# Gates ahead of q and k in the first projections of a two-layer retention trunk

## The chip, the cores and the metric

The kernel runs on one core of a Trainium2 chip. The core has a matrix engine (PE, with its weight loads listed apart as PEld), a vector engine (DVE), a scalar engine (ACT), a general engine (POOL) and an engine that issues the transfers (SP). They run their own instruction lists and wait for each other through semaphores. Matmuls write to PSUM, which has eight banks of 128 x 512 float32.

The metric is the time of one execution on the device, in microseconds. The kernel before takes 1574.14 us, the median of three runs (1573.3 to 1576.88).

## The reference, cut to what matters

Two layers over 512 tokens with 1024 channels. The part in which the change lies is the first layer's input projection and the retention behind it:

```python
h = modulate(rmsnorm(x, norm1[l]), sh1, sc1)
proj = h @ w_in[l]
q, k, v, g_sw, p_in, gates = jnp.split(proj, IN_SPLITS, axis=-1)
q = rotary(q.reshape(bsz, s, RET_HEADS, RET_QK_DIM), cos, sin)
k = rotary(k.reshape(bsz, s, RET_HEADS, RET_QK_DIM), cos, sin)
v = v.reshape(bsz, s, RET_HEADS, RET_V_DIM)
ret = head_rmsnorm(retention_chunkwise(q, k, v)).reshape(bsz, s, RET_V)
ret_d = (jax.nn.silu(g_sw) * ret) @ w_ret_o[l]
# ... the pooling branch, the merge, the output projection and the feed-forward part
```

There are 8 heads with 64 channels of q and k and 128 channels of v and of `g_sw`. In the kernel "gate" means a 128-column tile of `g_sw`, one for each head, with its SiLU. A 128-column tile of q or k holds two heads.

## The kernel before, in words

**Numbers and tiles.** Every float32 matrix product is done as three products of a split form: each operand is a high part (`whi` for weights) and a low part (`wlo`), and high x high, low x high and high x low are summed in PSUM (`mm3`). A weight chunk is 128 x 1024 (eight units of 128 x 128); it is fetched into `raw` (4 buffers), cast to `whi` and subtracted to `wlo` (5 buffers each). `ps()` takes one of the 8 PSUM banks. `h` holds the eight normalised input tiles, `tab` (4 buffers) the cosine and sine tables of the rotary step, `t` temporaries, `r` longer-lived tiles.

**The first projections** (`start`, line 670). While the modulation rows of layer 0 still arrive, the loop over the eight input tiles k makes `h[k]`, fetches weight chunk k and adds its products into eight PSUM banks at once: two tiles of q, two of k and four gates (`N_GATES`). Within one k the eight tiles are written one after another, in the order of the list `cols`, once for each of the three products. All eight banks are taken when the loop ends.

**What follows it.** For head group g = 0 (heads 0 to 3) the program runs through q pair 0, q pair 1, k pair 0, k pair 1: `tile_of` hands out the PSUM tile, `rotary` (line 750) copies it out in four 32-row pieces on ACT (`COPY t<-ps`), multiplies the bank by the cosine table on DVE (`t<-ps,tab`), multiplies the copy by the sine table and adds. Then each half is cast to `r` on ACT and the rest is subtracted on DVE. The four gates come after that: one `ACTIVATE r<-ps` with SiLU each (`gate`, line 788). Then the v projection (`vp`, line 820) takes four banks at once and runs 8 x 4 x 3 = 96 matmuls over them; in the trace these are `ps<-whi,h` and `ps<-wlo,h`. Then, head by head, the scores (`ps<-r,r` and `ps<-ql,r`), the projection of the gate of a later head, and the product with v (`ps<-s,r`).

**What sets the order.** The body only records operations; `Recorder.order` then plays a list schedule. Matmuls keep the order in which they were recorded. On the other engines it takes what is ready, by due times that it works out backwards from the matmuls that need a result and from the next user of a buffer. A PSUM bank is given to the tiles in the order of their first use, and each new tile takes the bank that comes free first. The planner also decides which of DVE and POOL, or of ACT and DVE, runs some operations. Each engine then executes its list strictly in that order, with SP's list of transfers among them. Accesses of two engines to the same PSUM bank are kept apart by semaphores in the order of that plan, reads too.

Since every operation is emitted by one line, the profile calls all of them L384; tiles are told apart by name.

Of the kernel before, what the change touches and what calls it, by code (L numbers as in the profile page):

```python
# [14 lines left out]
P = 128  # L15
# [4 lines left out]
HEADS = 8  # L20
# [13 lines left out]
C_G = C_V + D  # L34
# [14 lines left out]
N_GATES = 4  # L49
# [346 lines left out]
def trunk(ctx, tc, xT, cin, wada, vecs, wst, rot, trid, icnt, out):  # L396
# [8 lines left out]
    def ps():  # L405
        return nc.tile(pp, [P, S], F32, "ps", 8)
# [64 lines left out]
    def unit(l, name, k, col, n=1):  # L471
        key = (l, name, k, col)
        if key not in order:
            for q in range(n):
                order[(l, name, k, col + q * P if n > 1 else col)] = len(order)
        c, o = divmod(order[key], UNITS)
        for cc in range(c, c + look[0] + 1):
            prep(cc)
        sl = slice(o * P, (o + n) * P)
        return his[c][:, sl], los[c][:, sl]  # L480

    def mm3(out_ap, w, a, start, stop):

        (wh, wl), (ah, al) = w, a
        for n, (s, m) in enumerate(((wh, ah), (wl, ah), (wh, al))):
            nc.tensor.matmul(out_ap, lhsT=s, rhs=m, start=start and n == 0, stop=stop and n == 2)
# [10 lines left out]
    def hs(h, sl):  # L497
        return tuple(z[:, sl] for z in h)
# [20 lines left out]
    def mod_tile(l, t):  # L519

        w = raw_tile()
        nc.sync.dma_start(out=w, in_=wada[l, t])
        nc.vector.scalar_tensor_tensor(
            out=w, in0=w, scalar=1.0, in1=cact, op0=ALU.mult, op1=ALU.mult, accum_out=mods[l][:, t:t + 1],
        )

    def mod_bias(l, t0, n):
        m, b0 = mods[l], V_B + l * 48 + t0
        nc.vector.tensor_add(out=m[:, t0:t0 + n], in0=m[:, t0:t0 + n], in1=vec[:, b0:b0 + n])
# [56 lines left out]
    def make_h(l, which, k, sl, h):  # L586

        hh, hl = (z[:, sl] for z in h)
        sh = mods[l][:, (0 if which == 1 else 24) + k:][:, :1]
        t = temp()[:, sl]  # L590
        nc.vector.scalar_tensor_tensor(
            out=t, in0=x[k][:, sl], scalar=gains[l, which][:, k:k + 1], in1=rs[:, sl], op0=ALU.mult, op1=ALU.mult)
        nc.add({
            "scalar": ("activation", (hh, t, AF.Identity), dict(bias=sh)),
            "vector": ("tensor_scalar", (), dict(out=hh, in0=t, scalar1=sh, scalar2=None, op0=ALU.add)),
        })
        nc.vector.scalar_tensor_tensor(
            out=hl, in0=t, scalar=sh, in1=hh.bitcast(F32), op0=ALU.add, op1=ALU.subtract)

    def new_h():  # L600
        return [tuple(nc.tile(ap, [P, S], F32R, "h", N_H) for _ in range(2)) for _ in range(KT)]

    def first_tiles(l, which, h, name, cols, norm_b):

        o = [ps() for _ in cols]
        for sl in (A, B):
            for k in range(KT):
                for t, c in zip(o, cols):
                    mm3(t[:, sl], unit(l, name, k, c), hs(h[k], sl), k == 0, k == KT - 1)
                if sl is A and k == STAT_AT:  # L610
                    norm_b()
                    for kk in range(KT):
                        make_h(l, which, kk, B, h[kk])
        return o
# [31 lines left out]
    h = new_h()  # L646
# [7 lines left out]
    def first_norm():  # L654

        ss = [(sl, ps()[:, sl]) for sl in (A, B)]
        for n in range(N_WARM):
            nc.tensor.matmul(ss[1][1][:, :P], lhsT=ones, rhs=ones, start=True, stop=True)
        silu_c()
        q = []  # L660
        for k in range(KT):
            q.append(square(k))
            if 0 < k < KT - 2:
                nc.vector.tensor_add(out=q[0], in0=q[0], in1=q.pop())
        for sl, o in ss:
            for n in range(3):
                nc.tensor.matmul(o, lhsT=ones, rhs=q[n][:, sl], start=n == 0, stop=n == 2)
        return ss

    def start(cols):  # L670

        ss = first_norm()
        o = [ps() for _ in cols]
        for k in range(KT):
            mod_tile(0, 8 + k)
            mod_tile(0, k)
            mod_bias(0, k, 1)
            mod_bias(0, 8 + k, 1)
            gain(0, 1, k, 1)
            prep(k, 2 if k == 0 else 1)  # L680
            for sl in (A, B) if k == 0 else (FULL,):
                if k == 0:
                    rstd(rs[:, sl], dict(ss)[sl], D)
                make_h(0, 1, k, sl, h[k])
            nc.urgent = False
            if k + 1 == KT:
                look[0] = LOOK
            for sl in (A, B) if k == 0 else (FULL,):
                for n, (a, b) in enumerate(((0, 0), (1, 0), (0, 1))):
                    for t, c in zip(o, cols):  # L690
                        nc.tensor.matmul(t[:, sl], lhsT=unit(0, "in", k, c)[a], rhs=h[k][b][:, sl],
                                         start=k + n == 0 and sl.start != S // 2, stop=k + n == KT + 1)
        nc.sync.dma_start(out=ic, in_=icnt)
        nc.sync.dma_start(out=tri, in_=trid)
        return o

    def qk_cols(t):

        g, r = divmod(t, 4)
        is_k, pair = divmod(r, 2)  # L700
        return is_k * RQK + (2 * g + pair) * P
# [58 lines left out]
    norm_b = None  # L760
    for l in range(DEPTH):
# [2 lines left out]
        gates = {}  # L764
        p0 = {}
        if l == 0:
            done = start([qk_cols(t) for t in range(4)] + [C_G + n * P for n in range(N_GATES)])
        else:
            done = first_tiles(l, 1, h, "in", [qk_cols(t) for t in range(3)], norm_b)
        fill = [("gate", n) for n in range(len(done) - 4 if l == 0 else 0, HEADS)] + [("pool", g) for g in (3, 2, 1, 0)]  # L770

        def tile_of(col, mid=None):
            if done:
                return done.pop(0)
            o = ps()
            project(o, l, "in", col, h, mid=mid)
            return o
# [10 lines left out]
        def gate(hd):  # L788
            gp = tile_of(C_G + hd * P)
            gates[hd] = keep(F32)  # L790
            nc.scalar.activation(gates[hd], gp, AF.Silu)

        for g in range(2):

            parts = []
            for is_k in (0, 1):
                for p in range(2):
# [6 lines left out]
                    o = rotary(pr, tab)  # L804
# [10 lines left out]
                            nc.vector.tensor_sub(out=ql[own], in0=o[own], in1=z[own].bitcast(F32))  # L815
                            parts.append([z, ql])

            for n in range(len(done)):
                gate(n)
            vp = [ps() for _ in range(4)]  # L820
            for k in range(KT):
                wv = unit(l, "in", k, C_V + g * 512, 4)
# [5 lines left out]
            for i in range(4):  # L828
# [4 lines left out]
                for j in range(4):  # L833
                    c0 = min(j, 2) * P
                    w = S - c0
                    o = sp[min(j, 2)][:, w * (j == 3):w * (j == 3) + w]
# [41 lines left out]
        for j in range(KT):  # L878
            o = ps()
# [17 lines left out]
        for j in range(KT):  # L897
# [6 lines left out]
            t = temp()  # L904
# [15 lines left out]
        norm_b = close(l, "out", 0, merged, 16, STAT_TILES["out"], half_a)  # L920


        done = first_tiles(l, 2, h2, "ffn_in", [0, FF, P], norm_b)
# [19 lines left out]
        if l + 1 < DEPTH:  # L943
# [3 lines left out]
            h = new_h()  # L947
# [18 lines left out]
        norm_b = close(l, "ffn_out", HALF_FT, hid, 40, STAT_TILES["ffn_out"], half_a, l + 1 == DEPTH)  # L966
# [69 lines left out]
```

## Time and profile before

| what | value |
|---|---|
| median of three runs | 1574.14 us (1573.3 to 1576.88) |
| the profiled execution's own time | 1580.4 us |
| its span, first to last instruction | 1578.6 us |
| PE busy | 1537.1 us (97%), 7302 matmuls |
| DVE, ACT, POOL busy | 894.2 (57%), 557.5 (35%), 168.9 us (11%) |
| mean granted PE clock | 0.988 |
| DMA | 201.18 MB, mean 127 GB/s |

The span is the time from the first to the last instruction of one profiled execution; 1.8 us of its own time lie outside the span, and the execution was 6.3 us slower than the median of the runs. A busy share is an average over the whole program; a place where PE stands still is seen in the views by stretch of time. In rows of the timeline the first two numbers are the start and the duration in us, `x8` is the number of instructions merged into the row, and a bracket gives the idle time before it and what ended that. PEclk is the clock that PE was granted, 1.00 being full speed.

### The profile page before, as it was taken

To read this page: it belongs to the slowest core of one execution; us is meant where nothing else is said; L and a number is where in the kernel's file an instruction comes from. 1 tells how busy PE (TensorE), PEld (TensorE's weight loads), DVE (VectorE), ACT (ScalarE), POOL (GpSimd) and SP (SyncE) were. 2 spreads that over 40 slices of the span, in tenths; PEclk is the share of its full clock that TensorE was granted. 3 is DMA by queue.
4 is the path that set the end of the run, shared out by engine and by line. 5 is a ranking of instruction groups with operands and counts; after the bars stand their busy time and mean duration, and the time that the engine had idled before them with its cause. 6 is when DMAs were issued, how large, how long until landed. Compare 5 with 4: busy or idle time off the path is not lost.

```text
span 1578.6 us, 18373 instructions
## 1 busy us (share of the span) xinstructions
PE 1537.1 (97%) x7302; PEld 1280.5 (81%) x7302; DVE 894.2 (57%) x1284; ACT 557.5 (35%) x784; POOL 168.9 (11%) x130
## 2 busy tenths in 40 slices
PE   7899999999999999999999999999999999999997
PEld 5678878888988888888898888888889888888887
DVE  8957785377485434654377766546747433333344
ACT  3355653232342222222256666223224322122222
POOL 2211351000010000000021323100002000000000
PEclk8989999999999999999999999999999999999999
DMA  7742424466245434564224232445622333332321
GB/s 242 253 138 64 149 58 145 152 200 195 70 146 163 142 94 147 187 189 155 84 75 154 80 107 67 147 146 186 202 94 74 101 96 102 96 93 94 94 67 54
DMA packets 59305, 201.18 MB, mean 127 GB/s; under 512 B 6609, under 2 KB 8913, under 8 KB 59218
## 3 DMA queue, kind: packets, MB, share of 16 engines
q1 hardware_dynamic: 59218, 200.00, 40.1%
q8 instruction: 57, 0.93, 0.2%
q14 instruction: 30, 0.25, 0.0%
HBM read 197.87 MB, written 2.10 MB: 127 GB/s over the span
## 4 chain that ended last, share of the span: by engine, by line
PE 91%; DVE 6%; ACT 1%; DMA 1%; issue 1%; DVEq 0%; SPq 0%; ACTq 0%
PE ps L384 91%; DVE t L384 3%; DVE raw L384 1%; DVE h L384 1%; ACT t L384 1%; DMA xall<-xT 0%; DVE r L384 0%; DVE mod L384 0%; DMA raw<-wst 0%; DVE acc L384 0%; DVE xall L384 0%; DVE s L384 0%; ACT whi L384 0%; DVE rs L384 0%; DVE wlo L384 0%
## 5 line engine op out<-in xcount | busy, mean ns | idle before, releaser
L384 PE MATMUL ps<-h,whi 128*128 128x512 f32 (+1 forms) x2720 | 812.6, 382 | 14.4 <-DVE h L384 11.6
L384 PEld LDWEIGHTS ps<-h,whi 128*128 128x128 f32 x2720 | 502.0, 189 | 117.0 <-DVE h L384 11.4
L384 DVE TENSOR_TENSOR wlo<-raw,whi 128x1024 fp32r<-128x1024 f32 (+1 forms) x233 | 290.3, 1248 | 380.7 <-ACT whi L384 380.0
L384 PE MATMUL ps<-h,wlo 128*128 128x512 f32 (+1 forms) x1360 | 504.5, 379 | 0.0
L384 ACT CAST whi<-raw 128x1024 fp32r<-128x1024 f32 (+1 forms) x239 | 250.4, 1048 | 688.9 <-PE ps L384 486.3
L384 PE MATMUL ps<-r,whi 128*128 128x512 f32 (+1 forms) x1620 | 442.3, 357 | 0.0
L384 PEld LDWEIGHTS ps<-r,whi 128*128 128x128 f32 x1620 | 286.9, 188 | 46.6
L384 PEld LDWEIGHTS ps<-h,wlo 128*128 128x128 f32 x1360 | 255.8, 189 | 49.5
L384 PE MATMUL ps<-r,wlo 128*128 128x512 f32 (+1 forms) x810 | 288.1, 356 | 0.0
L384 PEld LDWEIGHTS ps<-r,wlo 128*128 128x128 f32 x810 | 152.2, 188 | 23.0
L384 POOL TENSOR_TENSOR wlo<-raw,whi 128x1024 fp32r<-128x1024 f32 x29 | 72.9, 2517 | 620.0 <-DVE rs L384 329.1
L384 DVE SCALAR_TENSOR_TENSOR raw<-raw,cact 128x1024 f32<-128x1024 f32 x96 | 122.4, 1277 | 13.6 <-DMA raw<-wada 13.1
L384 PE MATMUL ps<-whi,h 128*128 128x512 f32 x256 | 83.5, 408 | 8.6 <-ACT t L384 8.6
L384 DVE TENSOR_TENSOR t<-ps,t 128x512 f32<-128x512 f32 x60 | 41.3, 688 | 78.9 <-PE ps L384 78.2
L384 DVE SCALAR_TENSOR_TENSOR xall<-ps,mod,xall 128x512 f32<-128x512 f32 (+1 forms) x62 | 39.0, 628 | 71.8 <-PE ps L384 71.8
L384 ACT ACTIVATE t<-ps 128x512 f32<-128x512 f32 x76 | 45.0, 595 | 89.9 <-PE ps L384 89.9
L384 PEld LDWEIGHTS ps<-whi,h 128*128 128x128 f32 x256 | 49.3, 194 | 22.6 <-ACT t L384 10.9
L384 DVE TENSOR_TENSOR r<-t,r 128x512 fp32r<-128x512 f32 (+1 forms) x76 | 56.2, 740 | 5.3 <-ACT r L384 3.3
L384 ACT CAST r<-t 64x512 fp32r<-64x512 f32 (+1 forms) x84 | 51.6, 617 | 18.8 <-DVE t L384 16.0
L384 PE MATMUL ps<-wlo,h 128*128 128x512 f32 x128 | 51.8, 405 | 0.0
L384 ACT ACTIVATE sq<-xall 128x256 f32<-128x256 f32 (+1 forms) x42 | 20.5, 488 | 85.2 <-DVE xall L384 79.5
L384 ACT COPY t<-ps 32x512 f32<-32x512 f32 (+1 forms) x72 | 41.5, 578 | 25.2 <-PE ps L384 18.2
(89 smaller groups left out, 848.8 us busy)
## 6 DMA issues: line engine op xcount, KB each, us to landing
raw<-wst SPq DMA_DIRECT2D x261, 512.0 KB, 3.6
raw<-wada SPq DMA_DIRECT2D x96, 512.0 KB, 4.1
tab<-rot SPq DMA_DIRECT2D x32, 256.0 KB, 3.7
xall<-xT SPq DMA_DIRECT2D x4, 512.0 KB, 6.7
out<-t SPq DMA_DIRECT2D x7, 256.0 KB, 2.4
out<-t SPq DMA_DIRECT2D x2, 128.0 KB, 2.3
tri<-trid SPq DMA_DIRECT2D x1, 128.0 KB, 4.7
vec<-vecs SPq DMA_DIRECT2D x1, 72.0 KB, 7.7
```

The source lines that it names most:

```text
L384: getattr(eng, method)(*[real(a) for a in args], **{k: real(v) for k, v in kw.items()})
```

## The change

The list of columns in `start` begins with the four gates, and the two tiles of q and two of k follow. `start` returns a dictionary by column instead of a list, so that `tile_of` finds each tile by its column. The gates that `start` made are handled before the loop over head groups, so ahead of the rotary steps of q and k, where before they stood between the rotary steps and the v projection. In layer 1, which has no gates among its first tiles, only the bookkeeping changes. Nothing that is computed changes, and neither does the number of matmuls, transfers or SiLU calls.

```diff
@@ start
-        return o
+        return dict(zip(cols, o))
@@ trunk, at the head of each layer
         if l == 0:
-            done = start([qk_cols(t) for t in range(4)] + [C_G + n * P for n in range(N_GATES)])
+            done = start([C_G + n * P for n in range(N_GATES)] + [qk_cols(t) for t in range(4)])
         else:
-            done = first_tiles(l, 1, h, "in", [qk_cols(t) for t in range(3)], norm_b)
-        fill = [("gate", n) for n in range(len(done) - 4 if l == 0 else 0, HEADS)] + [("pool", g) for g in (3, 2, 1, 0)]
+            cols = [qk_cols(t) for t in range(3)]
+            done = dict(zip(cols, first_tiles(l, 1, h, "in", cols, norm_b)))
+        fill = [("gate", n) for n in range(N_GATES if l == 0 else 0, HEADS)] + [("pool", g) for g in (3, 2, 1, 0)]
 
         def tile_of(col, mid=None):
-            if done:
-                return done.pop(0)
+            if col in done:
+                return done.pop(col)
...
+        for n in range(HEADS):
+            if C_G + n * P in done:
+                gate(n)
         for g in range(2):
...
-            for n in range(len(done)):
-                gate(n)
             vp = [ps() for _ in range(4)]
```

How the instruction lists differ is seen at two places. In the rows below a name is tile, buffer and a running number: `ps_4` is PSUM bank 4, and the bracket names the engines or transfer queues whose semaphores the instruction waits for.

The first is ACT just after its last weight cast for the v projection. `ps_4` to `ps_7` are the four tiles that `start` takes first (the q and k tiles before, the gates now), `ps_1`, `ps_2`, `ps_3` and `ps_0` the other four. Before:

```order
L384 CAST whi_1_572<-raw_3_550 128x1024 [waits DMAHW2_49,PE_49,Pool_49]
L384 COPY t_7_596<-ps_4_190 32x512 [waits PE_49]
L384 COPY t_7_596<-ps_4_190 32x512 [waits DVE_49]
L384 COPY t_7_596<-ps_4_190 32x512 x2
L384 COPY t_5_615<-ps_5_195 32x512 [waits PE_49]
L384 COPY t_5_615<-ps_5_195 32x512 [waits DVE_49]
L384 COPY t_5_615<-ps_5_195 32x512 x2
L384 COPY t_6_634<-ps_6_197 32x512 [waits PE_49]
```

And now:

```order
L384 CAST whi_1_570<-raw_3_548 128x1024 [waits DMAHW1_49,PE_49,Pool_49]
L384 ACT_TABLE_LOAD
L384 ACTIVATE r_0_596<-ps_4_190 128x512 [waits PE_49]
L384 ACTIVATE r_1_601<-ps_5_195 128x512 [waits PE_49]
L384 ACTIVATE r_2_606<-ps_6_197 128x512 [waits PE_49]
L384 ACTIVATE r_3_615<-ps_7_200 128x512 [waits PE_49]
L384 COPY t_7_623<-ps_1_202 32x512 [waits DVE_49,PE_49]
L384 COPY t_7_623<-ps_1_202 32x512
L384 COPY t_7_623<-ps_1_202 32x512 [waits DVE_49]
L384 COPY t_7_623<-ps_1_202 32x512
```

The table load and the four SiLU calls, which stood behind all 16 copies and all 12 casts of the rotary steps, now stand ahead of them; the rotary pieces moved behind.

The second is PE at the first matmuls of the v projection. Before:

```order
L384 MATMUL ps_4_619<-whi_3_524,h_0_188 128x512 [waits DVE_49,Activation_49]
L384 MATMUL ps_4_619<-whi_3_524,h_1_211 128x512
L384 MATMUL ps_4_619<-wlo_3_562,h_0_188 128x512
L384 MATMUL ps_5_636<-whi_3_524,h_0_188 128x512 [waits DVE_49,PE_49,Activation_49]
L384 MATMUL ps_5_636<-whi_3_524,h_1_211 128x512
L384 MATMUL ps_5_636<-wlo_3_562,h_0_188 128x512
L384 MATMUL ps_6_653<-whi_3_524,h_0_188 128x512 [waits DVE_49,PE_49,Activation_49]
L384 MATMUL ps_6_653<-whi_3_524,h_1_211 128x512
L384 MATMUL ps_6_653<-wlo_3_562,h_0_188 128x512
L384 MATMUL ps_7_673<-whi_3_524,h_0_188 128x512 [waits PE_49,Activation_49]
```

And now:

```order
L384 MATMUL ps_4_608<-whi_3_522,h_0_188 128x512 [waits Activation_49]
L384 MATMUL ps_4_608<-whi_3_522,h_1_211 128x512
L384 MATMUL ps_4_608<-wlo_3_560,h_0_188 128x512 [waits DVE_49]
L384 MATMUL ps_5_618<-whi_3_522,h_0_188 128x512 [waits Activation_49]
L384 MATMUL ps_5_618<-whi_3_522,h_1_211 128x512
L384 MATMUL ps_5_618<-wlo_3_560,h_0_188 128x512
L384 MATMUL ps_6_628<-whi_3_522,h_0_188 128x512 [waits Activation_49]
L384 MATMUL ps_6_628<-whi_3_522,h_1_211 128x512
L384 MATMUL ps_6_628<-wlo_3_560,h_0_188 128x512
L384 MATMUL ps_7_633<-whi_3_522,h_0_188 128x512 [waits Activation_49]
```

The banks are the same four, but their former content is now a gate, which one SiLU on ACT reads, and no longer a q or k tile, which four copies on ACT and a product on DVE read. The order of the matmuls themselves is the same in the whole program but for the tiles that change places within `start`. On ACT, DVE, POOL and SP the two lists differ only around the rotary steps and the first head of layer 0 (6 to 24 rows an engine); POOL has two instructions fewer, DVE two more.

## The prediction

> **What bounds the kernel now.** I read the page first, then what PE waits for, then stretches of time.
>
> ```profile
> span 1578.6 us, 18373 instructions
> PE 1537.1 (97%) x7302; PEld 1280.5 (81%) x7302; DVE 894.2 (57%) x1284; ACT 557.5 (35%) x784; POOL 168.9 (11%) x130
> ```
>
> PE is busy 97% of the span, so only places where PE stands still or runs slowly can give time. The waits of PE, as engine, tile, what was waited for, us in total, times, longest:
>
> ```profile
> PE ps L384 <- DVE h L384: 11.6, 9, 3.0
> PE ps L384 <- ACT t L384: 8.6, 4, 2.9
> ```
>
> The second row is what the change touches: four waits for a rotary copy. The view by stretch shows where it lies (columns: length, busy us and instructions of each engine, granted clock, DMA share, GB/s):
>
> ```profile
> core 0: us, PE busy (x) PEld busy (x) DVE busy (x) ACT busy (x) POOL busy (x), PEclk, DMA share, GB/s
> 57.00:73.20 16.20, 14.23 (x60) 10.75 (x59) 15.10 (x19) 5.83 (x6) 5.72 (x2) 1.00 0.86 271
> 73.10:76.03 2.93, 0.00 (x1) 0.00 (x0) 1.70 (x3) 1.75 (x4) 0.00 (x0) 1.00 0.88 316
> 76.03:91.21 15.18, 9.49 (x21) 6.28 (x22) 10.07 (x14) 12.61 (x22) 5.11 (x4) 0.55 0.72 236
> 91.21:108.70 17.49, 17.49 (x76) 14.03 (x75) 7.44 (x9) 8.70 (x13) 0.00 (x0) 1.00 0.30 91
> 108.70:117.66 8.96, 8.96 (x46) 7.50 (x44) 5.92 (x14) 3.35 (x7) 2.41 (x1) 1.00 0.20 59
> 131.00:200.00 69.00, 69.00 (x313) 56.39 (x311) 50.63 (x71) 41.39 (x66) 22.96 (x16) 1.00 0.35 107
> 228.00:235.00 7.00, 5.17 (x18) 4.37 (x19) 6.00 (x12) 4.03 (x8) 3.35 (x2) 0.76 0.25 75
> ```
>
> Between the last matmul of the first projections and the first score lies the v projection. Its first 15.18 us hold little work and run at a clock of 0.55; the rest runs full. The rows of PE there:
>
> ```profile
> 71.10 2.00 PE L384 MATMUL ps<-h,whi 128*128 128x512 f32 x8
> 76.03 0.74 PE L384 MATMUL ps<-whi,h 128*128 128x512 f32 x2 [2.93 <-ACT t L384]
> 79.14 1.22 PE L384 MATMUL ps<-whi,h 128*128 128x512 f32 x2 [2.13 <-ACT t L384]
> 82.25 1.22 PE L384 MATMUL ps<-whi,h 128*128 128x512 f32 x2 [1.46 <-ACT t L384]
> 85.99 1.22 PE L384 MATMUL ps<-whi,h 128*128 128x512 f32 x2 [2.09 <-ACT t L384]
> 107.31 0.63 PE L384 MATMUL ps<-whi,h 128*128 128x512 f32 x2
> 108.00 0.63 PE L384 MATMUL ps<-whi,h 128*128 128x512 f32 x2
> 108.70 0.39 PE L384 MATMUL ps<-r,r 128*128 128x512 f32 x1
> ```
>
> The first projections end at 71.10 + 2.00 = 73.10. Each of v's four banks is waited for separately, because its former q or k tile has to be copied out first. From 73.10 to the first score at 108.70 it takes **35.60 us**. At full clock three matmuls take 108.70 − 108.00 = 0.70 us (and 108.00 − 107.31 = 0.69), so v's 96 need 32 x 0.70 = 22.4 us. The other 13.2 us are idle time (8.61, the sum of the four brackets) and half clock (4.6).
>
> **The change part by part.** *Order inside the first projections.* The same eight tiles, weights and transfers for each k; the gates only end first. DVE and POOL set that loop's pace and their rows are the same. SP fetches three weight chunks ahead of one table now, which can only bring the weights earlier. I cost it at zero; its 73.10 stays.
>
> *The wait for v's banks.* ACT's rows (and one of each kind from the view by tile, as min/median/max ns):
>
> ```profile
> 71.29 1.05 ACT L384 CAST whi<-raw 128x1024 fp32r<-128x1024 f32 x1 [1.90 <-PE ps L384]
> 72.36 0.58 ACT L384 COPY t<-ps 32x512 f32<-32x512 f32 x1
> 74.23 2.35 ACT L384 COPY t<-ps 32x512 f32<-32x512 f32 x4 [1.29 <-DVE t L384]
> 94.21 1.28 ACT L384 ACT_TABLE_LOAD   x1
> 95.51 2.06 ACT L384 ACTIVATE r<-ps 128x512 f32<-128x512 f32 x4
> L384 ACT ACTIVATE r<-ps x4: 592/602/619, 95.5 to 97.0; 128x512 f32<-128x512 f32 x4
> L384 ACT COPY t<-ps x16: 574/577/580, 72.4 to 85.4; 32x512 f32<-32x512 f32 x16
> ```
>
> Before, a bank costs four copies of 0.58 and a DVE product in their midst, some 3.1 us. Now the load follows the cast at 72.36 and takes 1.28 with 0.02 to the next start (94.21 to 95.51); the four SiLU start every 0.5 us (95.5 to 97.0). The first ends at 72.36 + 1.30 + 0.60 = 74.26, the last at 73.66 + 2.06 = 75.72. PE needs 0.70 us for a bank's three matmuls, so after the first bank it meets no further wait: the four banks are wanted at 74.3, 75.0, 75.7, 76.4 and free at 74.3, 74.8, 75.2, 75.7. v runs from 74.3 to 74.3 + 22.4 = **96.7**, against 108.70: a gain of **12.0 us**, 1.7 at its start, 5.7 of later idle time and 4.6 of half clock.
>
> The Trainium skill (ScalarE: Activation LUTs, What ACT_TABLE_LOAD costs) counts about 1.28 us for the load and another 1.38 us of drain, 2.66 us a switch. The trace agrees with the load and shows no drain behind it (1.30 us from start to start); by the page v would start 1.4 us later and the gain be 10.6 us.
>
> *The clock over the gap that is left.* PE now idles 74.3 − 73.1 = 1.2 us. The nearest rows are two gaps in the first projections:
>
> ```profile
> 60.63 2.09 PE L384 MATMUL ps<-h,whi 128*128 128x512 f32 x8 [0.90 <-DVE h L384]
> 67.36 2.07 PE L384 MATMUL ps<-h,whi 128*128 128x512 f32 x8 [0.98 <-ACT whi L384]
> ```
>
> They are 0.9 and 1.0 us long and the clock stays 1.00 (stretch 57 to 73.2). So I cost it at nothing; the far bound is the whole of v's first 15.18 us at 0.55, which loses 0.45 x 15.18 = 6.8 us.
>
> *The rotary steps move behind.* Their 16 copies and 12 casts start on ACT at 75.7, not 72.4. What waits for them is the first score, at 96.7 now. For the four tiles, with the last weight subtraction for v ahead of them:
>
> ```profile
> 72.37 1.23 DVE L384 TENSOR_TENSOR wlo<-raw,whi 128x1024 fp32r<-128x1024 f32 x1 [0.96 <-ACT whi L384]
> 85.96 5.60 ACT L384 CAST r<-t 64x512 fp32r<-64x512 f32 x9
> 88.64 0.69 DVE L384 TENSOR_TENSOR ql<-t,r 64x512 fp32r<-64x512 f32 x1
> L384 DVE TENSOR_TENSOR t<-ps,tab x4: 683/690/691, 73.5 to 84.6; 128x512 f32<-128x512 f32 x4
> L384 POOL TENSOR_TENSOR t<-t,tab x3: 1276/1279/1287, 76.1 to 86.1; 128x512 f32<-128x512 f32 x3
> DMA to landing us min/median/max: 2.5/5.1/6.8
> 106.80 2.69 ACT L384 CAST r<-ps 128x512 fp32r<-128x512 f32 x4 [2.69 <-PE ps L384]
> 115.48 2.34 PE L384 MATMUL ps<-s,r 128*128 128x512 f32 x12
> ```
>
> v's weights are no new wait: their last cast ends at 72.34 and its low part at 72.37 + 1.23 = 73.6. ACT's list then does q pair 0, one piece of q pair 1, k pair 0. Two copies (to 76.9), DVE's product 0.69, two copies (78.8), one piece (79.4), three copies of k (81.1). DVE makes two products and a sum for q (81.5), then multiplies k's bank; that cosine table goes into the buffer that q's product freed at 77.6, so it lands between 80 and 84.4 (2.5 to 6.8 us). k's fourth copy, its sine product and its sum follow, then ACT's cast (0.62 us) and DVE's subtraction of 0.69: the first head's q and k are ready near 87, or near 90 with the slowest transfers. That is 7 to 10 us ahead of 96.7.
>
> The price comes behind that. From 75.7 on ACT has 16 copies (9.3), 12 casts (7.5) and two weight casts (2.1), 18.9 us, and I count 3 us of waits for DVE: it reaches v's casts at about 97.6, where before it stood ready when v's first bank ended (106.80, 1.9 us ahead of the score). DVE carries more too: two products that POOL did (1.28 us each there) and a cast of v. The first head's last score cast comes at about 102.2. The product with v starts 115.48 − 108.70 = 6.8 us after the first score, at 103.5. So the work is hidden, with 1.3 us to spare. Uncovered it costs what it is late, one for one. DVE's rotary product now stands behind a weight cast that waits for its transfer; what is behind it is the chain just counted.
>
> *Sum:* 35.6 − (1.2 + 22.4) = 12.0 us. Nothing later takes it back: the lists are the same from head 1 on, and PE is full there (69.00 of 69.00 us), so everything moves ahead by 12 us. The profiled execution took 1580.4 us and would take 1568.4; it was 6.3 us slower than the median of the runs, so I apply the difference to that: 1574.14 − 12.0 = **1562.1 us**.
>
> **The rivals.** *ACT's backlog shows* (12%). Between the first score and the product with v PE waits for the score casts. For it: 1.3 us to spare against some 22 us of work in two in-order lists that wait for each other. Against it: half of the casts and subtractions belong to heads 1 to 3. If ACT or DVE is 3 to 6 us later than counted, PE loses 2 to 5: 1564 to 1567 us.
>
> *The clock falls all the same* (6%). For it: in the stretch from 228 a few small gaps brought the clock to 0.76, so the threshold is not only the length of one gap. Its price is between a stretch like that (7.00 x 0.24 = 1.7 us) and 6.8: 1563.8 to 1568.9. The Trainium skill (TensorE: Matmul & The Clock Gate, A second HAM failure mode: psum-queue depth-cycling) says that many short pauses while banks are cycled can make the clock fall and recover; the row from 76.03 agrees with it, and this speaks against the kernel before more than against the change, since PE pauses once now.
>
> *Nothing is gained* (4%): the banks don't pass as said, or a later wait takes all back. The instruction lists speak against the first: v's four banks wait for ACT alone. Against the second stands that the next 69 us hold no wait of PE. It would give 1574.
>
> *Slower* (3%). The tables for k stand behind one weight chunk more in SP's list, and each needs a buffer that an earlier rotary product frees; DVE executes in order, so one late table holds up q, k, the weight subtractions and v's split together. It decides when the first head's q and k come after 108.7 instead of 87: then each us more is a us lost, and a chain ending at 112 gives 1574.1 + 3.3 = 1577.4. Three transfers in a row at the slowest 6.8 us only reach 90 to 93, so it would need a stall that no row shows.
>
> **How the numbers follow.** The forecast, 12.0 us gained within about 2 us, has 75%. The stretches with a reduced clock elsewhere, such as the one from 228, cost 1.7 us each and may fall differently after a shift, so the likeliest case alone is 1559.5 to 1564. The range reaches to the backlog and the cheaper half of the clock's fall: **1559 to 1567**. A measurement of this kernel tells about 0.2% (3 us) from no change. Faster by more: 75 + 12 + 6 = 93%. Within: the 4%, 4%. Slower by more: 3%.
>
> **What would show it.** In the changed kernel's profile: the table load and four SiLU right after the cast that ends near 72.3; PE's idle time before v's first matmul 1.0 to 1.4 us and none before the next three banks; the clock 1.00 through v; the first score near 96.7; no wait of PE for `ACT t`; copies and casts of the rotary steps lasting to about 96 on ACT. It is wrong if the first score is reached near 96.7 but PE then waits for `s` or `r` (the backlog), if v's matmuls are spaced by 0.4 us and more instead of 0.70 / 3 = 0.23 (the clock), or if the score comes late, with q or k named as the wait.

## The result and the profile after

The changed kernel takes 1563.97 us (median, 1562.12 to 1567.92) where the kernel before took 1575.41 us on the same chip (1573.3 to 1577.67): a ratio of 0.9925 with a 95% interval of 0.9909 to 0.9941, so 11.8 us of 1575. A second, longer comparison of the same two kernels gave 1565.59 against 1574.71 us, 0.9937 (0.9918 to 0.9956), or 9.9 us. The forecast was 1562.1 us, with 12.0 us gained.

The profiled execution took 1567.9 us. Its page, the rows on the span and the engines:

```profile
span 1566.1 us, 18369 instructions
PE 1532.0 (98%) x7302; PEld 1276.6 (82%) x7302; DVE 897.1 (57%) x1286; ACT 557.0 (36%) x784; POOL 169.4 (11%) x128
```

The waits of PE over the whole program, those that answer to the two rows shown of before:

```profile
PE ps L384 <- DVE h L384: 13.4, 11, 2.9
PE ps L384 <- ACT r L384: 0.9, 1, 0.9
```

The wait for `ACT t` (four times, 8.6 us) is gone. One wait for `ACT r`, a gate's SiLU, is there in its place, 0.9 us long. The view by stretch, from v's start to the first score, and from there to that of the second head:

```profile
core 0: us, PE busy (x) PEld busy (x) DVE busy (x) ACT busy (x) POOL busy (x), PEclk, DMA share, GB/s
74.30:96.70 22.40, 22.33 (x96) 18.02 (x97) 18.31 (x24) 19.82 (x34) 1.31 (x1) 1.00 0.65 221
96.70:105.70 9.00, 9.00 (x46) 7.50 (x44) 7.78 (x15) 4.80 (x10) 4.82 (x2) 1.00 0.53 166
```

v's 96 matmuls now lie in one stretch of 22.4 us that is full, at a clock of 1.00; before, the first 15.18 us held 21 of them at 0.55. The 9 us behind it, in which the backlog would have shown, are full too. ACT is busy 19.82 of v's 22.40 us: the rotary work did move there. PE's rows:

```profile
71.51 1.99 PE L384 MATMUL ps<-h,whi 128*128 128x512 f32 x8
74.37 0.73 PE L384 MATMUL ps<-whi,h 128*128 128x512 f32 x2 [0.87 <-ACT r L384]
...
75.17 0.63 PE L384 MATMUL ps<-whi,h 128*128 128x512 f32 x2
...
96.88 0.40 PE L384 MATMUL ps<-r,r 128*128 128x512 f32 x1
...
103.68 2.32 PE L384 MATMUL ps<-s,r 128*128 128x512 f32 x12
105.83 0.39 PE L384 MATMUL ps<-r,r 128*128 128x512 f32 x1
```

One bracket is left, of 0.87 us; the second bank at 75.17 has none. From 73.50 (71.51 + 1.99) to the first score at 96.88 it takes **23.38 us**, against 35.60 before: 12.2 us less. From the first score to that of the second head it takes 105.83 - 96.88 = 8.95 us, as before (8.96). ACT's rows:

```profile
71.36 1.05 ACT L384 CAST whi<-raw 128x1024 fp32r<-128x1024 f32 x1 [1.86 <-DMA raw<-wst]
72.43 1.28 ACT L384 ACT_TABLE_LOAD   x1
73.72 2.07 ACT L384 ACTIVATE r<-ps 128x512 f32<-128x512 f32 x4
...
96.91 1.56 ACT L384 CAST r<-ps 128x512 fp32r<-128x512 f32 x3
...
99.89 1.03 ACT L384 CAST s<-ps 128x384 fp32r<-128x384 f32 x3
```

The table load starts 0.02 us after the weight cast, and the four SiLU follow. ACT comes to v's casts at 96.91. The chain of waits of the changed kernel passes through the same place:

```profile
66.13 5.13 DMA raw<-wst
71.36 1.05 ACT whi L384
72.43 1.28 ACT L384
74.37 38.44 PE ps L384 x172
```

So what starts v is now the last weight chunk's transfer, its cast, the table load and one SiLU, in a row on ACT.

The stretches ahead of layer 1's last phase show that nothing is taken back. PE's rows at two events there, in the kernel before and in the changed one:

```profile
806.81 0.50 PE L384 MATMUL ps<-h,whi 128*128 128x256 f32 x2 [1.58 <-DVE h L384]
...
1200.68 0.50 PE L384 MATMUL ps<-h,whi 128*128 128x256 f32 x2 [1.44 <-DVE h L384]
```

```profile
794.60 0.51 PE L384 MATMUL ps<-h,whi 128*128 128x256 f32 x2 [1.59 <-DVE h L384]
...
1188.38 0.50 PE L384 MATMUL ps<-h,whi 128*128 128x256 f32 x2 [1.44 <-DVE h L384]
```

The lead is 12.2 us at the first of these events, 12.3 at the second and 12.5 at the end of the span (1578.6 - 1566.1). At the first score it is 108.70 - 96.88 = 11.8 us, because the first projections ended 0.4 us later in this execution.

### The profile page after: what moved, and what is told of

Read it like the earlier page. It is cut to its first block, busy times and chain, and to the rows that moved or that the text cites. A ratio compares the mean times of both kernels' runs of the same rounds, so it can differ in the third digit from the quotient of the medians.

```text
span 1566.1 us, 18369 instructions
## 1 busy us (share of the span) xinstructions
PE 1532.0 (98%) x7302; PEld 1276.6 (82%) x7302; DVE 897.1 (57%) x1286; ACT 557.0 (36%) x784; POOL 169.4 (11%) x128
## 4 chain that ended last, share of the span: by engine, by line
PE 92%; DVE 6%; DMA 1%; ACT 1%; issue 0%; POOL 0%; SPq 0%; DVEq 0%; ACTq 0%
PE ps L384 92%; DVE t L384 2%; DVE raw L384 1%; DVE h L384 1%; DMA raw<-wst 1%; DMA xall<-xT 1%; DVE r L384 0%; DVE mod L384 0%; DVE xall L384 0%; DVE acc L384 0%; POOL wlo L384 0%; ACT t L384 0%; DVE s L384 0%; ACT whi L384 0%; ACT sq L384 0%
## 5 line engine op out<-in xcount | busy, mean ns | idle before, releaser
L384 POOL TENSOR_TENSOR wlo<-raw,whi 128x1024 fp32r<-128x1024 f32 x30 | 77.4, 2583 | 603.2 <-DVE rs L384 329.4
L384 DVE SCALAR_TENSOR_TENSOR raw<-raw,cact 128x1024 f32<-128x1024 f32 x96 | 120.8, 1260 | 12.1 <-DMA raw<-wada 11.8
L384 PEld LDWEIGHTS ps<-whi,h 128*128 128x128 f32 x256 | 48.0, 188 | 12.9 <-ACT r L384 1.3
```

Source lines behind the costliest of these rows:

```text
L384: getattr(eng, method)(*[real(a) for a in args], **{k: real(v) for k, v in kw.items()})
```

## The experiments

Below, "the stretch" is the time from the end of the first projections to the first score, as above: 35.60 us before, 23.38 us with the change. It is read from one profiled execution, where one wait can be told from another; the total time can't resolve less than some 3 us here. Executions of the same instruction lists differ in the stretch too, by up to 0.7 us: it is 35.60 and 34.89 us with the lists of the kernel before, and 23.38, 23.41 and 23.01 us with those of the change (the runs follow below).

### Which part of the change does it

The columns alone: the gates are handled where they stood before, and only the order of the columns is changed.

```diff
-        for n in range(HEADS):
-            if C_G + n * P in done:
-                gate(n)
         for g in range(2):
...
+            for n in range(HEADS):
+                if C_G + n * P in done:
+                    gate(n)
             vp = [ps() for _ in range(4)]
```

> Only the order of the columns is changed; the gates are recorded where they stood before, between the rotary steps and the v projection. Theory: what counts is which tiles sit in the four PSUM banks that v gets, and the planner puts the SiLU calls early by itself because v's first matmuls want those banks: first score at 96.9 us, ratio to the kernel before 0.9925 (0.991 to 0.994), no wait of PE for a rotary copy. Rival: the earlier place of the gate calls is what helps; then v waits for rotary copies as before, first score near 108.7, ratio 1.000.

The instruction lists of all engines came out as those of the change, row for row. The stretch is 23.41 us, as the theory has it. The time is 1571.24 us, against 1576.24 before, 0.9949 (0.9925 to 0.9973), with executions from 1563.5 to 1572.0; the ratio lies outside the theory's 0.991 to 0.994, but its interval reaches the 0.9925. The profiled one has a span of 1565.4 us.

The calls alone: the gates are handled first, and the columns are in the old order.

```diff
-            done = start([C_G + n * P for n in range(N_GATES)] + [qk_cols(t) for t in range(4)])
+            done = start([qk_cols(t) for t in range(4)] + [C_G + n * P for n in range(N_GATES)])
```

> The other part of the change alone: the gates are recorded ahead of the rotary steps, but the columns keep their old order (q, q, k, k, then the gates). Theory: v's banks are still those of the q and k tiles, the planner puts the SiLU calls back behind the rotary work, and the instruction lists are those of the kernel before: ratio 1.000 within 0.002, four pauses ahead of v's banks. It is also a second look at the kernel before: if the half clock after such pauses depends on where they happen to fall, the stretch from the first projections to the first score differs from the 35.6 us of the first profile by up to 2 us; if it follows from the lists alone, it is 35.6 again. Rival: the earlier calls are worth something by themselves: SiLU ahead of the rotary copies, stretch of 30 us or less, ratio below 0.998.

The lists came out as those of the kernel before, the time is 1575.41 against 1575.05 us, 1.0001 (0.9985 to 1.0017), and the stretch 34.89 us with the same four waits. PE's first row of v:

```profile
76.92 1.22 PE L384 MATMUL ps<-whi,h 128*128 128x512 f32 x2 [3.14 <-ACT t L384]
```

In the kernel before, the first two matmuls of v took 0.74 us and only the later ones were slow; here the first two are slow already. So with the same lists the clock fell at another place among the matmuls, and the stretch differs by 0.7 us.

So the order of the columns is the whole change: it decides which tiles sit in the banks that v takes first. Where the calls stand in the program is of no effect, because the planner places them by due times.

Two gates first: an order between the two kernels, so that v's first two banks held gates and the next two q tiles.

```diff
-            done = start([C_G + n * P for n in range(N_GATES)] + [qk_cols(t) for t in range(4)])
+            done = start([C_G, C_G + P] + [qk_cols(t) for t in range(4)] + [C_G + 2 * P, C_G + 3 * P])
```

> The columns in the order gate, gate, q, q, k, k, gate, gate: two of v's four banks held gates, two hold q tiles. Theory: a gate's bank costs v 0.5 us, a q tile's bank four copies and a product, 3.1 us: the third bank is free at 78.4, the fourth at 81.5, and 87 matmuls are left: first score at 101.8 with the full clock, up to 104.2 if the two pauses bring half clock for some 5 us; 1568.5 to 1571. Rival: it is enough that the SiLU calls no longer stand behind all the rotary work: first score near 97, 1564. Rival on the other side: one rotary bank among the four is enough to lose all: 108, 1575.

```profile
74.21 0.73 PE L384 MATMUL ps<-whi,h 128*128 128x512 f32 x2 [1.47 <-ACT r L384]
...
77.81 0.73 PE L384 MATMUL ps<-whi,h 128*128 128x512 f32 x2 [1.93 <-ACT t L384]
...
80.92 1.22 PE L384 MATMUL ps<-whi,h 128*128 128x512 f32 x2 [2.15 <-ACT t L384]
```

The two banks with gates pass with one wait, each bank with a q tile brings one of 2 us, and the clock falls again (the two matmuls at 80.92 take 1.22 us, those at 74.21 took 0.73). The stretch is 30.77 us, 4.8 less than before, and the time 1572.08 us, 0.997 (0.9954 to 0.9986), 4.7 us less. The first score comes at 103.51 us, between the 101.8 and 104.2 that the theory gave; both rivals fail. The gain goes bank by bank.

### What the half clock costs, and what brings it

Fillers on part of the array: the kernel before, with 9, 8 and 10 more matmuls in v's first three banks that add zero to them, to fill PE's waits. Their stationary and moving operands have 64 rows, and the first is all zero.

```diff
+N_ZERO = (9, 8, 10)
...
+                    if l + g + k == 0 and t < 3:
+                        for _ in range(N_ZERO[t]):
+                            nc.tensor.matmul(vp[t], lhsT=q_low[0][64:128, :P], rhs=h[0][0][64:128], start=False, stop=False)
```

> The kernel before, with 9, 8 and 10 extra matmuls by a zero operand into v's first, second and third bank, placed in the pauses between v's first matmuls: PE has work while it waits for the rotary copies, and the sums don't change. Theory: the waits for the banks stay (last bank near 86.0) and are the larger part; only the half clock goes, so the 87 matmuls that are left run at 0.233 us, first score at 86.0 + 20.3 = 106.3, 2.4 us earlier than before: 1573 against 1575.4. Rival: the half clock costs its whole 4.6 us on top of the pauses: first score at 104.1, 1571. Third: matmuls by zeros don't keep the clock up; then it stays at 0.55 and the first score comes at 108.7 or later.

The time is 1585.68 us, 1.005 (1.0028 to 1.0072): slower. PE by stretch (length, busy us and instructions, granted clock, DMA share, GB/s):

```profile
core 0: us, PE busy (x), PEclk, DMA share, GB/s
79.00:82.00 3.00, 3.00 (x8) 0.50 0.87 284
91.00:94.00 3.00, 3.00 (x8) 0.50 0.00 0
```

In both stretches PE is full and is still granted half its clock. The fillers are too many at that clock and the stretch grows to 42.64 us: the third of the outcomes that were considered. It tells nothing on v's waits, but a filler that doesn't hold the clock up leaves two possibilities, zeros or the part of the array.

Fillers on the whole array: 4, 3 and 4 matmuls over 128 rows, on real data; the bank is cleared by v's first product behind them, so they are work without use.

```diff
+N_FILL = (4, 3, 4)
...
+                    if l + g + k == 0 and t < 3:
+                        for _ in range(N_FILL[t]):
+                            nc.tensor.matmul(vp[t], lhsT=h[0][0][:, :P], rhs=wv[0], start=True, stop=True)
```

> The kernel before, with 4, 3 and 4 extra matmuls ahead of v's first product in its first three banks; they multiply real data over all 128 rows, and the first product of the bank then overwrites them. All other lists are those of the kernel before. Theory: the clock follows how much PE really works; PE is busy through the pauses now, so the clock is at 1.00 some 4 us after v's start (from about 80 on), and from the last bank (86.0) on the 87 matmuls that are left take 20.3 us: from the end of the first projections to the first score 33.2 us against 35.6 before. Rival: the half clock follows from the pause of about 3 us alone and lasts whatever follows; then it is still 0.5 at 86 to 91, and the stretch takes 35.6 us or more.

A single execution took 1574.27 us. PE's rows and its view by stretch (columns as above):

```profile
71.72 2.02 PE L385 MATMUL ps<-h,whi 128*128 128x512 f32 x8
76.72 2.93 PE L385 MATMUL ps<-whi,h 128*128 128x512 f32 x6 [2.97 <-ACT t L385]
...
86.70 0.73 PE L385 MATMUL ps<-whi,h 128*128 128x512 f32 x2 [1.85 <-ACT t L385]
...
107.10 0.39 PE L385 MATMUL ps<-r,r 128*128 128x512 f32 x1
```

```profile
76.70:79.70 3.00, 2.98 (x7) 0.50 0.30 68
80.00:82.00 2.00, 1.49 (x7) 1.00 1.02 367
```

The clock falls once, behind the pause of 2.97 us that no filler covers, and is back at 1.00 by 80, though v's banks still come free one by one. The stretch is 33.36 us: 2.2 less than before, where the theory gave 33.2. And the last bank comes free no sooner: v's fourth bank starts 86.70 - 73.74 = 12.96 us after the first projections, where before it was 85.99 - 73.10 = 12.89. So the clock does not set when the banks pass on; ACT and DVE do.

The same fillers with a tile of 128 x 128 zeros as the stationary operand:

```diff
+    zero_r = nc.tile(cp, [P, P], F32R, "zero_r")
+    nc.gpsimd.memset(zero_r.bitcast(F32), 0.0)
...
+                            nc.tensor.matmul(vp[t], lhsT=zero_r, rhs=wv[0], start=True, stop=True)
```

> The same with the stationary operand all zeros, still over all 128 rows. Where the earlier filler used zeros on 64 rows, the clock stayed at 0.50 for 17 us. If it is the zeros that don't count as work, the clock stays at 0.5 until 4 us after the last filler (beyond 90) and the stretch from the first projections to the first score takes 35.6 us or more. If it was the half-used array that didn't count, zeros on 128 rows keep the clock as real data do: 33.2 us.

```profile
78.00:80.00 2.00, 2.00 (x5) 0.50 0.88 323
...
82.00:84.00 2.00, 1.43 (x6) 0.90 0.98 335
```

The clock comes back, near 82.4, and the stretch is 32.63 us. (The single execution took 1580.89 us, a total that this stretch does not explain; the last section says where it comes from.) So zeros by themselves do not keep the clock down. What failed was 64 rows, or 64 rows with zeros; the two were not told apart.

A longer pause ahead of v: the changed kernel, with the first gate's SiLU computed three times, and five times.

```diff
-            nc.scalar.activation(gates[hd], gp, AF.Silu)
+            for _ in range(3 if l + hd == 0 else 1):
+                nc.scalar.activation(gates[hd], gp, AF.Silu)
```

> The changed kernel with the first gate's SiLU computed three times, so that v's first bank comes free about 2.0 us later and PE pauses for about 2.4 to 2.9 us ahead of v instead of 0.9. Theory: one pause shorter than some 3.4 us does not lower the clock; v then takes its 22.4 us, and from the end of the first projections to the first score it is 25.0 us (23.4 in the changed kernel, plus what the pause has grown). Rival: the pause by itself brings half clock for some 5 us, as the four pauses did before: 27.5 us.

```profile
74.70 0.73 PE L384 MATMUL ps<-whi,h 128*128 128x512 f32 x2 [1.91 <-ACT r L384]
75.51 1.05 PE L384 MATMUL ps<-whi,h 128*128 128x512 f32 x2
```

```profile
core 0: us, PE busy (x), PEclk, DMA share, GB/s
72.06:75.47 3.41, 1.50 (x7) 1.00 1.02 399
75.47:78.88 3.41, 3.41 (x9) 0.50 0.39 116
```

The pause grew to 1.91 us, not to the 2.4 to 2.9 that were planned, and this was enough for 3.4 us at half clock (by 79 it is 1.00 again). The stretch is 25.96 us, 2.58 more than with the change: 1.04 from the pause and some 1.5 from the clock. My theory that the clock survives a single pause of this length fell; the rival had the fall right, but not its 5 us.

> The changed kernel with the first gate's SiLU computed five times: v's first bank comes free about 4 us later and PE pauses for about 4.3 to 4.8 us. Theory: a pause beyond some 3.4 us lowers the clock to one half for about 4 us of work, which costs another 2 us: from the end of the first projections to the first score 4.5 + 22.4 + 2 = 28.9 us. Rival: the clock doesn't fall after a single pause of this length: 26.9 us.

With five SiLU the pause grew only to 2.25 us, not to the length that I had planned, and the clock was at half from 76.4 to 79.9; the stretch is 26.41 us, 3.03 more than with the change: 1.38 from the pause and 1.65 from the clock. It confirms the event and its price, and says nothing on pauses beyond 3.4 us.

### Is the rotary work hidden with room to spare

More work for ACT: the changed kernel, with the eight casts of the heads' halves of q and k in group 0 made twice, and three times (8 and 16 more casts of some 0.62 us on ACT, which change no value).

```diff
-                        nc.scalar.copy(out=z[own], in_=o[own])
+                        for _ in range(2 if l + g == 0 else 1):
+                            nc.scalar.copy(out=z[own], in_=o[own])
```

(`range(3 if ...)` in the second.)

> The changed kernel with each of the eight high-part casts of the first rotary steps done twice on ACT, 5.0 us more of ACT work behind the SiLU calls; the planner moves some weight casts away from ACT. What the changed kernel leaves is 103.68 - 100.92 = 2.8 us between the last score cast of the first head and the product with v. Theory (ACT's backlog is what comes next): the 5.0 us eat that margin, and PE waits 0 to 2 us for the first head's casts. Rival: the 11 us between the first head's q and k (85.8) and the first score (96.9) are the margin, and nothing is lost: first projections to the second head's scores 32.3 us as in the changed kernel.

From the end of the first projections to the second head's scores it takes 33.64 us, 1.3 more than with the change, but 1.0 of this is a longer pause ahead of v. The first head, from its first score to that of the second, takes 9.27 us, 0.3 more. (The single execution took 1563.37 us.) This run shows another thing by the way:

```profile
75.11 0.73 PE L384 MATMUL ps<-whi,h 128*128 128x512 f32 x2 [1.86 <-ACT r L384]
...
75.91 0.63 PE L384 MATMUL ps<-whi,h 128*128 128x512 f32 x2
```

Here a pause of 1.86 us left the clock at 1.00: the second bank's two matmuls take 0.63 us, where they took 1.05 after the pause of 1.91. The clock changes only at points 3.41 us apart (the last section has the evidence), and one of them, at 74.96, lies within this pause. PE in the windows on its two sides (columns as above):

```profile
71.55:74.96 3.41, 1.70 (x8) 1.00 0.99 381
74.96:78.38 3.42, 3.27 (x14) 1.00 0.51 207
```

The pause of 1.91 us lay in one window whole and left PE 1.50 us of work in it; this one is shared by two and leaves 1.70 and 3.27.

> The same with each cast done three times, 9.9 us more of ACT work. Theory (backlog): 9.9 - 2.8, less some 2 to 4 us of weight casts that move to DVE, is 3 to 5 us of waiting by PE around the first head, 35 to 37 us from the end of the first projections to the second head's scores. Rival: still hidden, 32.3 us.

```profile
104.59 0.72 PE L384 MATMUL ps<-s,r 128*128 128x256 f32 x2 [0.34 <-DVE s L384]
```

PE now waits a little within the product with v. (The run with three SiLU calls has a wait of 0.37 us at the same place without any added cast.) The first head takes 9.72 us, 0.8 more than with the change, and from the end of the first projections to the second head's scores it takes 32.62 us, close to the rival's 32.3. (The single execution took 1562.03 us.) The theory of a backlog with little room expected 35 to 37 us. One reservation: the planner rearranged ACT's list, and rotary casts of later heads now stand behind the casts of v's banks. So it shows that the work can be hidden, through the planner's moves as well, more than it measures the spare time of the changed kernel's own list.

### The wait that is left

The table load ahead of time: the changed kernel, with one SiLU of a 128 x 1 column (its result is not used) during the first projections, so that the table is there already.

```diff
+            if k == 3:
+                nc.scalar.activation(eps_t[:, 1:], h[3][0][:, :1].bitcast(F32), AF.Silu)
```

> The changed kernel plus one tiny SiLU of a 128x1 column during the first projections, so that the SiLU table is already there when the gates are done. Theory: v's start (74.37) is held by the last weight cast, the table load of 1.28 and the first SiLU, in that order on ACT; without the load the first bank is free at about 73.1, before PE ends the first projections (73.5), so PE's pause of 0.87 us goes and the first score comes 0.9 us earlier, at 96.0: 1563 us if the changed kernel has 1564 in the same runs. Rival: something else, such as the weights of v, holds the start; then PE still pauses and the first score stays at 96.9.

```profile
70.37 2.00 PE L384 MATMUL ps<-h,whi 128*128 128x512 f32 x8
72.21 0.62 PE L384 MATMUL ps<-whi,h 128*128 128x512 f32 x2
```

The pause is gone: v's first row has no bracket. The stretch is 22.23 us, 1.15 less than with the change (0.9 was the pause itself). The time of 1567.76 us, 0.9942 (0.9921 to 0.9963), can't tell this from the change. In the profile it is the better kernel by 0.8 to 1.2 us in that stretch, against the three executions with the change's lists; in time no difference was measured.

The change once more, as it is:

> The changed kernel as it is, in more rounds, since the kernel with the same instruction lists (columns alone) gave a ratio of 0.9949 with a wide interval. Theory: the gain is the 12 us of the v projection, ratio 0.9925 (0.991 to 0.994), and what differs between the runs is not in these lists. Rival: a part of the gain is lost in many runs somewhere later; then the ratio is near 0.995 again.

The time is given above: 0.9937, inside the theory's 0.991 to 0.994. Its interval of 0.9918 to 0.9956 still holds the rival's 0.995, so the time alone does not decide between the two. The pause was 0.50 us in its profiled execution and the stretch 23.01 us, with the same lists: how late the last weight cast comes, measured against the end of the first projections, differs from execution to execution by some tenths.

## Why the prediction was right, and where it was off

**The start of the first projections costs nothing.** They end at 73.50 in the profiled execution of the change (73.10 before), and at 73.29 (71.30 + 1.99 in PE's rows) in the repeated one. That is within the spread: with the lists of the change they end at 71.76 in the run with the columns alone, and with those of the kernel before at 73.78 in the run with the calls alone.

**The banks.** Load and SiLU came as worked out: the load at 72.43 (72.36 in the working), the four SiLU from 73.72 (73.66), no wait at the next three banks. The pause is 0.87 us where 1.2 was worked out, because the matmuls ahead of it ended 0.4 us later; it lies just below the 1.0 to 1.4 us that the prediction named as its sign. The Trainium skill (ScalarE: Activation LUTs, What ACT_TABLE_LOAD costs) gives 1.28 us for a load, which the row at 72.43 has to the digit, and a drain of 1.38 us besides, which has no room here: the load starts 0.02 us after the cast ahead of it, and from its start to that of the first SiLU it is 73.72 - 72.43 = 1.29 us. The lower price, and with it 12 and not 10.6 us, was the right one.

**v at full clock.** 96.88 - 74.37 = 22.5 us against 22.4, and the first score at 96.88 against 96.7.

**The split of the gain** is the step that explains less than it seemed to. The sum 1.7 + 5.7 + 4.6 counts time as it is seen on PE, and it comes out right since all of it goes. But its parts are not causes that could be taken away one by one. With the clock held up and the banks as before, 2.2 us were gained and not 4.6: at half clock PE works longer on a bank and then waits less for the next. What the kernel before lost was first the 12.9 us in which four q and k tiles are read by ACT and DVE in turns, and then some 2.3 us of half clock behind the last of them, of which the fillers show the size.

**The clock over the pause that is left.** Costing it at nothing was right (1.00 through v), but its reason was incomplete. It leaned on pauses of 0.9 and 1.0 us, as if the length of a pause decided; what decides is how much of a fixed window of 3.41 us PE stands still (last section). The remark under the rivals, that the threshold is not only the length of one gap, was the better lead. In the changed kernel the pause lies in this one (PE busy, granted clock, DMA share, GB/s):

```profile
73.02:76.44 3.42, 2.55 (x12) 1.00 1.02 405
```

PE is busy for 75% of it, and falls were seen only up to 54%. The far bound of 6.8 us was too far for a single pause: one fall costs about 1.6 us, as the two runs with a longer pause show, or nearly half of the 3.41 us that it lasts.

**The rotary work behind.** It is hidden, as forecast. The first head's last score cast ended at 99.89 + 1.03 = 100.92, not 102.2, and the product with v came at 103.68 (103.5): 2.8 us to spare instead of 1.3. I had counted some 3 us of waits of ACT for DVE on its path; its rows between 75.8 and 96.9 have 2.2 us (0.76, 1.21 and 0.20), and it reached v's casts at 96.91 instead of 97.6. The 2.8 us are ACT's side alone: DVE's subtractions for the first two score tiles, which the product needs as well, end at 101.5 in its rows, 2.1 us ahead of it.

**Nothing later takes it back.** The lead of 11.8 us at the first score is 12.3 us at 1188 and 12.5 at the end. The half clock elsewhere did fall differently, as the prediction allowed: the kernel before has it from 231.1 and from 1203.9 for 3.4 us each, the changed kernel at neither place but from 428.0. Where the starts of the same matmuls are compared in the two traces, each of these moves the lead by 0.3 to 0.8 us, and not by the 1.7 that was counted. In the total, 11.8 and 9.9 us were measured, and 8.0 us in the run with the same lists and other source text; the intervals of the first two reach 12 us, that of the third ends at 11.8 ((1 - 0.9925) x 1576). What differs between executions by some microseconds lies elsewhere, as the last section shows. So it is partly luck that the profiled execution came so close (1567.9 us against 1568.4 worked out): it and the profiled execution before both had the slower matmuls described there, 4.4 us that some other executions lack.

**The rivals.** A backlog of ACT: not seen, and 0.8 us under some 10 us of added casts (16 x 0.62). A fall of the clock in v: not seen, but nearer than thought. Nothing gained, and late tables for k: ruled out by the first score at 96.88 and by the first head's 8.95 us.

## What to carry to other kernels

When an accumulation is to start in PSUM banks that others must read first, look at who reads them: a bank with one reader is free after one instruction (0.5 us a gate here), while a bank that two engines read in turns holds it for several (3.1 us a q or k tile). Put the quickly read tiles where the next accumulation takes its banks, and the slowly read ones where the result is needed late; the order in which tiles are first allocated can be all it takes, and the order of the calls nothing. And count a stall by what a filled or shortened version of it gives, since idle time and slow clock of the same stretch are not independent.

## What was not expected of the hardware

**The clock changes at fixed points, and a half-idle window is enough.** The trace records every change of the granted clock. In each of the 14 profiled executions all changes lie on one grid of 3.41 us, and the place of this grid differs from execution to execution; until PE's work ends, each stretch at half clock lasts 3.41 us or two, four or six times that. Cut along the grid from 35 us to shortly before the end, the 14 traces hold 6179 windows at full clock, of which 26 were followed by half clock. Where PE was busy for less than 47% of the window the clock fell every time (20 of 20), between 47 and 54% in 6 of 28 cases, and above 54% never (0 of 6131). So the same pause can pass or not: with the same lists, a pause of 1.43 us at 217 left PE 2.06 us of work in its window of 3.41 in the changed kernel and the clock stayed, while in its repetition the same pause and the smaller ones next to it left 1.74, and the clock was 0.50 from 218.1 to 221.5. As an estimate from these shares, a lone pause below some 1.5 us is too short for a fall, one beyond some 3.6 us always suffices, and between them its place in the grid decides. The Trainium skill (TensorE: Matmul & The Clock Gate, HAM oscillation — how this bites in real kernels) asks for no idle gap above about 3.4 us. The length of the slow stretch, 3.41 us behind the pause of 1.91, agrees with that figure; the pause that suffices does not. The same page (What's actually happening) has the clock set by a window that runs on freely; the grid, at another place in each execution, agrees with that.

**Matmuls over 64 rows with a zero operand did not bring the clock back:** it was 0.50 from 76.0 to 96.5 with PE full, against 3.4 us with 128 rows of real data and 6.8 us with 128 rows of zeros. Whether they count in part or not at all, and whether 64 rows of real data would do, the runs don't show.

**The spacing of matmuls at full clock differs between executions.** The lists of the kernel before and of the calls alone are the same, and the latter's profiled execution was 5.9 us shorter. Of this, 4.4 us lie between two events of layer 1, whose rows in the calls alone are

```profile
805.33 0.50 PE L384 MATMUL ps<-h,whi 128*128 128x256 f32 x2 [1.58 <-DVE h L384]
...
1194.76 0.50 PE L384 MATMUL ps<-h,whi 128*128 128x256 f32 x2 [1.44 <-DVE h L384]
```

or 389.43 us, against 393.87 before (1200.68 - 806.81) and 393.78 with the change. PE has no idle time to speak of and a clock of 1.00 there. Matmul by matmul, the two executions keep step until about 970 us, drift apart by 0.38 us in every 20 until 1200, and keep step again. The two largest groups of instructions in the midst of that stretch (1010 to 1180), with one shape in each group, in the kernel before and in the calls alone:

```profile
L384 PE MATMUL ps<-r,whi 128*128 128x512 f32 x248 | 80.7, 397 | 0.0
L384 PE MATMUL ps<-h,whi 128*128 128x512 f32 x227 | 74.0, 397 | 0.0
```

```profile
L384 PE MATMUL ps<-r,whi 128*128 128x512 f32 x244 | 78.0, 391 | 0.0
L384 PE MATMUL ps<-h,whi 128*128 128x512 f32 x224 | 71.7, 391 | 0.0
```

All matmuls of this shape are slower there by the same amount: their starts lie 233.3 ns apart in the one and 228.9 in the other, 1.9% more. The wider spacing is seen in other runs too. The fillers with zeros over 128 rows have it here and around 260 to 400 us as well (397 ns a matmul, where the fillers with real data have 390), and these two stretches add 3.5 and 4.5 us to the one, where its whole span is 6.6 us longer. The cause of the wider spacing stays open. Its effect is as large as a third of the change's gain, and it is why the stretch, not the total, was used to compare the experiments.
